# Two blocks on one core: the first modulation sums on TensorE, the levels of the linear attention on VectorE, and another distance between hT and the weights

## Chip, cores and metric

One core of one Trainium2 chip. The metric is the time on the device for one execution, in microseconds (us); it is given as the median of several runs. All weights are read from HBM in each execution, 228 MB of them.

## What is computed

256 tokens of width 1024 pass through two blocks. The first block is modulated by a condition vector; the second has a gated linear attention and a differential attention. Cut to what the change touches:

```python
mod = silu(cond) @ w_mod + b_mod                 # 1024 -> 9 * 1024
sh1, sc1, g1, sh2, sc2, g2, sh3, sc3, g3 = split(mod, 9)
h = rms_norm(x, ffn1_norm) * (1 + sc1) + sh1
x = x + 0.5 * g1 * (silu(h @ w_gate) * (h @ w_up)) @ w_down      # FFN1
# mixer: gated short convolution beside a state-space model (SSM); FFN2
proj = rms_norm(x, a_norm) @ w_in                # linear attention, 4 heads
q, k, v, g, z = split(proj)
log_a = log_sigmoid(z @ w_gate_up + b_gate) / 16
b = cumsum(log_a) within chunks of 64
# o_i = sum over j <= i of (q_i * exp(b_i - b_j)) . k_j  v_j, with a state between chunks
x = x + (rms_norm(o) * silu(g)) @ w_out
# then MLP, differential attention, MLP
```

Everything is float32.

## The kernel before

**Weights.** A stream (`Stream`) takes the weights in one fixed order, in pieces of 1 MB. Three stage buffers receive them by DMAs that SyncE issues; a piece that is consumed lets the next DMA go. `prep` splits a piece into two parts, so that a product of float32 values is made of three fast matmuls (`mm3`): ScalarE casts `wh` (L170, two halves), VectorE subtracts it to get `wl` (L172, two halves). The activations are split in the same way into `hTh` and `hTl` (L276, L277). The pairs lie in four slots and a fifth one (`grow`). `prep(upto, items)` prepares pieces as far as slots are free; `take(name, j, ahead)` prepares up to the piece asked for and `ahead` more, by default as many as slots allow. Instructions stand on each engine in the order in which the code emits them.

**The w_mod pieces.** They are in the same stream, four to each of the nine groups, the first eight (shift and scale of FFN1) ahead of all other weights. `mod_part` adds them on VectorE into `macc` (L839, L841: one input row times a scalar of `cact`, added; two for each piece). `mod_reduce` then sums `macc` over the partitions by eight matmuls with a column of ones (L862), and two small VectorE steps put bias and gain to it (`modf`).

**The start.** The x rows are normalised and transposed (`xnT`, L335); `evac` scales and shifts them with `modf` (L364 on ScalarE, L366 on VectorE) and splits them into hT. `turn` then makes FFN1's first gate and up products with tokens on the output's partitions, 24 matmuls for each of two pieces and two token halves; the rest of FFN1 (`up`, then `acc` for the down products) runs with the hidden units on the partitions. Beside that GpSimd works on the SSM (`powers`, `readout`, `tables`), and `Ssm.step(s)` spreads what TensorE and ScalarE do for it over the steps s of FFN1.

**The linear attention (`gla`).** TensorE makes v by `turn`, z, four chunks of q and k (0 to 3, `featb`), the last chunk of v (7) and four gate chunks (8 to 11). From z come the gates: two matmuls each, then Abs, Exp and Ln on ScalarE, a subtraction and a scan on VectorE give `b`. Within a chunk of 64 the products are built by levels (1, 2, 4, 8, 16, 32): `level_e` subtracts `b` at block borders, `exp` follows on ScalarE, `level_x` scales q and k on VectorE, `level_mm` multiplies on TensorE and copies into `AT` by a mask. `diagonal` gives the diagonal; `across_e` and what follows join the chunks of 64.

**Addresses.** Tiles are placed one behind the other in each partition; `pad` tiles shift what comes behind them. The weights' slots lie at 96 bytes modulo 512; hT lies at 32 and q's hT (differential attention) at 160.

Of the kernel before, what the change touches and what calls it, by code (L numbers as in the profile page):

```python
# [193 lines left out]
class Net:  # L194
# [219 lines left out]
    def turn(self, tail, evac, chunks, use):  # L414
# [5 lines left out]
        if tail is None:  # L420
            evac(0)
            evac(1)
        else:
            for part in tail.parts[0]:
                part()
            tail.post(0)
            early = len(tail.parts[1]) - tail.late
            for part in tail.parts[1][:early - 2]:
                part()
            S.prep(S.n_take + n_c)  # L430
            for part in tail.parts[1][early - 2:early]:
                part()
            evac(0)
            for part in tail.parts[1][early:]:
                part()
            S.prep(S.n_take + n_c)
            tail.post(1)
            if self.after_tail is not None:
                self.after_tail()
                self.after_tail = None  # L440
                S.prep(S.n_take + n_c)
        Ws = []
        for i in range(2):
            for c in range(n_c):
# [7 lines left out]
                if i == 0 and c == 1 and n_c > 2:  # L452
                    evac(1)
# [110 lines left out]
class Ssm:  # L564


    def __init__(self, N, p):
# [136 lines left out]
    def step(self, s):  # L704
# [3 lines left out]
        if 2 <= s <= 4:  # L708
            for b in ((0, 1), (2, 3, 4), (5, 6, 7))[s - 2]:
# [6 lines left out]
            if s == 4:  # L716
                self.readout()
                self.tables()
# [64 lines left out]
def build(N):  # L783
# [64 lines left out]
    def mod_reduce(g, new_bank, later=False):  # L848
# [15 lines left out]
        def finish():  # L864
            col = modf[:, 2 * blk + kind, :]
            nc.vector.tensor_tensor(out=col, in0=bank[:, 0:KD], in1=sv["b_mod"][:, g, :], op=ADD)
            if kind == 1:
                nc.vector.scalar_tensor_tensor(out=col, in0=col, scalar=1.0, in1=(G_FFN1, G_MIX, G_FFN2)[blk], op0=ADD, op1=MUL)

        if later:  # L870
            return finish
        finish()
# [28 lines left out]
    mod_reduce(1, lambda: N.bank_a("mod"))  # L901
    ssm.powers()
# [32 lines left out]
    def side1(s):  # L935
# [4 lines left out]
    tail = N.ffn(None, lambda i: N.evac_mod(pts[i], i, modf[:, 1, :], modf[:, 0, :], N.hT),  # L940
                 ("ffn1_w_gate", "ffn1_w_up"), "ffn1_w_down", 11, True, post_ffn1, side1, 1)
# [327 lines left out]
def gla(N, tail, evac, c):  # L1269
    nc, t, t2, take = N.nc, N.t, N.t2, N.take  # L1270
    ones, misc, ident = c["ones"], c["misc"], N.ident
    vt, gt, act = nc.vector.tensor_tensor, nc.gpsimd.tensor_tensor, nc.scalar.activation
# [28 lines left out]
    wz = [v3(w, KD) for w in take("a_z")]  # L1301
# [6 lines left out]
    def featb(ch, dst, scale):  # L1308
        ps = N.bank_u("qk")
        N.feat(take("a_in", ch), N.hT, v3(ps, 2))  # L1310
        N.S.free()
        act(out=flat(dst), in_=ps, func=AF.Copy, scale=scale)

    qT, kT = t2([4, S], "qT"), t2([4, S], "kT")
    featb(0, qT[:, 0:2, :], 128 ** -0.5)
    gp = []
    for h2 in range(2):
        ps = N.bank_a("gate")
        for k in range(2):
            h = 2 * h2 + k  # L1320
            nc.tensor.matmul(ps[:, S * k:S * k + S], wgu[:16, 128 * h:128 * h + 128], zT[:16, :], start=True, stop=True)
        gp.append(ps)
# [18 lines left out]
    def level_e(li):  # L1341
# [6 lines left out]
        gt(out=ev[:, :, 1, :], in0=bv[:, :, 1, :], in1=ref, op=SUB)  # L1348
        gt(out=ev[:, :, 0, :], in0=ref, in1=bv[:, :, 0, :], op=SUB)
# [51 lines left out]
    def across_e():  # L1401
# [62 lines left out]
    W = take("a_in", 8)  # L1464
    level_x(2)
    level_e(4)
    exp(Es[4])
    level_x(3)
    level_e(5)
    exp(Es[5])  # L1470
    gate_chunk(0, W)
    level_mm(2)
    level_mm(3)
    W = take("a_in", 9)
# [42 lines left out]
    for hp in range(2):  # L1517
        for i in range(2):
            av(i, hp)
    for hd in range(3):  # L1520
        gated(hd)
    nc.scalar.preload_act_table(AF.Silu)
    W = take("a_in", 11)
    ps = N.bank_u("vg")
    for i in range(2):
        N.tokm(W, N.hT, i, ps[:, CW * i:CW * i + CW])
    N.S.free()
    act(out=flat(sg[3]), in_=ps, func=AF.Silu)
# [63 lines left out]
def diff(N, tail, c):  # L1592
# [149 lines left out]
    def turn_o(p):  # L1742
# [8 lines left out]
        else:  # L1751
            if p == 2:
                N.pad("pad_tail", 128, N.pool2)
# [140 lines left out]
```

## Time and profile before

| | us |
|---|---|
| median of 3 runs | 1246.31 |
| the three runs | 1244.81 to 1246.57 |
| the profiled execution, its own time | 1243.52 |
| its span in the trace | 1241.8 |
| TensorE busy in it | 1140.0 |
| VectorE busy | 796.8 |
| ScalarE busy | 613.7 |
| GpSimd busy | 237.1 |

The span runs from the first to the last instruction; the execution's own time has 1.7 us more around it. Busy time of engines overlaps. A line number stands for the code that emits an instruction, a helper's line for all its callers (L248 is `mm3`). A name with an arrow, as `turn<-wh,hTh`, is the output tile and the inputs; for a matmul `128*128 128x256` are the loaded block and the streaming operand. One float32 matmul with float32 operands leaves two records, of the split ones one.

### The profile page before, as it was taken

Reading aid. Unit: us, or ns where it says so; the run is one execution under the profiler, and the core shown is the slowest. Engines: PE = TensorE matmul, PEld = TensorE weight load, DVE = VectorE, ACT = ScalarE, POOL = GpSimd, SP = SyncE. Lnnn points to the kernel's source line nnn. Section 1 sums busy time; section 2 is a strip of 40 time slices with the busy share of each in tenths; the row PEclk is TensorE's granted clock in tenths of the full one; section 3 lists DMA queues with packets and bytes.
Section 4 is the critical chain, followed back from the end, with each engine's and each line's share of the span. In section 5 each row is a group of like instructions: output and inputs, shape, how many; then the busy total and the mean of one; then the engine's idle time right before and its main releaser. Section 6 shows DMA issues by size and latency. Waiting matters only on the chain.

```text
span 1241.8 us, 18751 instructions
## 1 busy us (share of the span) xinstructions
PE 1140.0 (92%) x7780; PEld 1055.1 (85%) x7780; DVE 796.8 (64%) x934; ACT 613.7 (49%) x941; POOL 237.1 (19%) x304
## 2 busy tenths in 40 slices
PE   2689999989788899999697998999999899999998
PEld 2678998979777889997697988999989898899997
DVE  7698788677877855454567656544468776545441
ACT  3444443564265544444473656555456665645541
POOL 8994399401400000000214100000000000000000
PEclk9989999999789999999897999999999899899999
DMA  8598788436243765563144255556435333455540
GB/s 319 205 326 310 270 321 325 149 136 238 94 177 137 281 235 180 174 233 105 68 149 158 73 182 204 177 200 203 170 136 200 107 136 119 173 193 180 180 157 34
DMA packets 33093, 230.13 MB, mean 185 GB/s; under 512 B 3680, under 2 KB 4064, under 8 KB 5872
## 3 DMA queue, kind: packets, MB, share of 16 engines
q1 hardware_dynamic: 31536, 224.05, 50.5%
q10 hardware_dynamic: 1472, 4.88, 1.1%
q8 instruction: 61, 1.00, 0.3%
q14 instruction: 24, 0.20, 0.0%
HBM read 227.87 MB, written 1.05 MB: 184 GB/s over the span
## 4 chain that ended last, share of the span: by engine, by line
PE 68%; DVE 15%; ACT 7%; POOL 4%; DMA 3%; issue 3%; ACTq 0%; DVEq 0%; POOLq 0%
PE acc L248 27%; PE up L248 25%; PE turn L248 8%; DVE wl L172 7%; PE kqv L248 2%; ACT wh L170 2%; POOL s_small L612 1%; PE xnT L335 1%; POOL s_small L615 1%; DVE macc L841 1%; PE lev L1370 1%; DMA stage<-in_w 1%; DMA stage<-in_a_in 1%; ACT s_lag L734 1%; PE glu L248 1%
## 5 line engine op out<-in xcount | busy, mean ns | idle before, releaser
L172 DVE TENSOR_TENSOR wl<-stage,wh 128x1024 fp32r<-128x1024 f32 x351 | 429.5, 1270 | 144.2 <-ACT wh L170 144.2
L170 ACT CAST wh<-stage 128x1024 fp32r<-128x1024 f32 x351 | 347.2, 1044 | 147.1 <-PE acc L248 37.5
L248 PE MATMUL up<-hTh,wh 128*128 128x256 f32 x1024 | 288.1, 281 | 0.2 <-ACT s_end L715 0.2
L248 PE MATMUL up<-hTl,wh 128*128 128x256 f32 x1024 | 287.0, 280 | 0.0
L248 PE MATMUL up<-hTh,wl 128*128 128x256 f32 x1024 | 286.9, 280 | 0.0
L248 PEld LDWEIGHTS up<-hTh,wl 128*128 128x128 f32 x1024 | 195.4, 191 | 0.0
L248 PEld LDWEIGHTS up<-hTh,wh 128*128 128x128 f32 x1024 | 192.5, 188 | 2.4 <-ACT s_end L715 0.5
L248 PEld LDWEIGHTS up<-hTl,wh 128*128 128x128 f32 x1024 | 192.4, 188 | 1.6 <-issue 0.2
L248 PE MATMUL acc<-wh,hidh 128*128 128x512 f32 x288 | 116.6, 405 | 10.7 <-ACT hidh L276 5.4
L248 PE MATMUL acc<-wh,hidl 128*128 128x512 f32 x288 | 116.1, 403 | 9.8 <-DVE hidl L277 9.5
L248 PE MATMUL acc<-wl,hidh 128*128 128x512 f32 x288 | 115.6, 401 | 1.7 <-DVE wl L172 1.7
L248 PE MATMUL turn<-wh,hTh 128*128 128x256 f32 x320 | 92.4, 289 | 10.2 <-ACT hTh L276 10.2
L248 PE MATMUL turn<-wl,hTh 128*128 128x256 f32 x320 | 91.6, 286 | 1.7 <-DVE wl L172 1.7
L248 PE MATMUL acc<-wh,macc 128*128 128x512 f32 x288 | 93.1, 391 | 0.0
L248 PE MATMUL turn<-wh,hTl 128*128 128x256 f32 x320 | 91.9, 287 | 0.0
L841 DVE SCALAR_TENSOR_TENSOR macc<-stage,cact,macc 128x1024 f32<-128x1024 f32 x63 | 85.5, 1358 | 4.1 <-DMA stage<-in_w_mod 2.6
L248 PEld LDWEIGHTS acc<-wh,hidl 128*128 128x128 f32 x288 | 55.9, 194 | 24.1 <-DVE hidl L277 11.6
L248 PEld LDWEIGHTS acc<-wh,hidh 128*128 128x128 f32 x288 | 55.9, 194 | 23.5 <-ACT hidh L276 6.3
L248 PEld LDWEIGHTS turn<-wh,hTh 128*128 128x128 f32 x320 | 62.5, 195 | 11.0 <-ACT hTh L276 10.8
L248 PEld LDWEIGHTS acc<-wl,hidh 128*128 128x128 f32 x288 | 55.9, 194 | 13.7 <-DVE wl L172 3.1
L248 PEld LDWEIGHTS turn<-wl,hTh 128*128 128x128 f32 x320 | 62.5, 195 | 2.1 <-DVE wl L172 1.9
L248 PEld LDWEIGHTS acc<-wh,macc 128*128 128x128 f32 x288 | 54.1, 188 | 11.0
(401 smaller groups left out, 2023.4 us busy)
## 6 DMA issues: line engine op xcount, KB each, us to landing
stage<-in_w SPq DMA_DIRECT2D x64, 1024.0 KB, 4.8
stage<-in_w_mod SPq DMA_DIRECT2D x36, 1024.0 KB, 5.0
stage<-in_ffn_w_gate SPq DMA_DIRECT2D x22, 1024.0 KB, 4.8
stage<-in_ffn_w_up SPq DMA_DIRECT2D x22, 1024.0 KB, 4.8
stage<-in_ffn_w_down SPq DMA_DIRECT2D x22, 1024.0 KB, 4.8
stage<-in_a_in SPq DMA_DIRECT2D x12, 1024.0 KB, 5.1
stage<-in_w_in SPq DMA_DIRECT2D x8, 1024.0 KB, 5.1
stage<-in_w_kv SPq DMA_DIRECT2D x8, 1024.0 KB, 4.9
```

Of the source, the lines that this page charges most:

```text
L170: nc.scalar.copy(out=h[:, b:e], in_=st[:, b:e])
L172: nc.vector.tensor_tensor(out=lo[:, b:e], in0=st[:, b:e], in1=h[:, b:e].bitcast(F32), op=SUB)
L248: self.nc.tensor.matmul(out, lhs(l, k), rhs(r, k), start=first and n == 0, stop=last and n == 3 * n_k - 1)
L335: self.nc.tensor.transpose(out, src, self.ident)
L612: g.tensor_tensor(out=o, in0=x, in1=y, op=op)
L615: g.tensor_scalar(out=o, in0=x, scalar1=s1, scalar2=s2, op0=op0, op1=op1)
L734: nc.scalar.copy(out=self.lag[32 * i:32 * i + 32, 4 * b:4 * b + 4, 32 * i:128], in_=ks[:32, :, 0:128 - 32 * i])
L841: nc.vector.scalar_tensor_tensor(out=acc, in0=wv[:, k, :], scalar=cc, in1=acc, op0=MUL, op1=ADD)
L1370: nc.tensor.matmul(ps[:, 64 * e:64 * e + 64], ks[:, 128 * e:128 * e + 128], qs[:, 64 * e:64 * e + 64], start=True, stop=True)
```

## The change

- **w_mod, groups 0 and 1.** `mod_part` makes 16 matmuls for each of the eight pieces: a 128x128 block of the piece is loaded, one column of `cact` streams, and each result goes to a column of its own in one PSUM bank (`early`). `mod_early` sums these columns on VectorE and puts bias and gain to them. The other seven groups stay as they are.
- **Order at the start.** Six of the eight pieces (four before) are emitted ahead of the transposes. The first gate and up pieces are prepared behind the first evacuation, the second evacuation stands behind the first 24 `turn` matmuls, and the SSM's powers behind that. The SSM's memsets go from GpSimd to VectorE. Its `s_end` transposes, read-out and tables come one step of FFN1 later.
- **Linear attention.** `level_e` and the differences of `across_e` go from GpSimd to VectorE, two copies of `across_e` to ScalarE. The gate matmuls stand between the two halves of chunk 0. `take(..., 0)` at six places prepares nothing ahead, and `prep` is called later. Levels are emitted in pairs. The last gate chunk is split into its token halves, one ahead of the `av` products and one behind them.
- **Addresses.** Other sizes of four pads put hT, and q's hT, at 352 modulo 512: 256 from the weights. They were 64 away (on either side).

The core of the diff:

```diff
     def mod_part(g, c, st):
         wv = v3(st, 2)
+        if g < 2:
+            if c == 0:
+                early[g] = N.bank_a("mod")
+            for j in range(KD):
+                for k in range(2):
+                    nc.tensor.matmul(early[g][:, j * 8 + 2 * c + k:j * 8 + 2 * c + k + 1], wv[:, k, 128 * j:128 * j + 128],
+                                     cact[:, 2 * c + k:2 * c + k + 1], start=True, stop=True)
+            return
...
+    def mod_early(g):
+        tot = t([KD], "rs_sq", bufs=2)
+        nc.vector.tensor_reduce(out=tot, in_=v3(early[g][:, 0:64], KD), axis=AX.X, op=ADD)
+        col = modf[:, g, :]
+        nc.vector.tensor_tensor(out=col, in0=tot, in1=sv["b_mod"][:, g, :], op=ADD)
+        if g == 1:
+            nc.vector.scalar_tensor_tensor(out=col, in0=col, scalar=1.0, in1=G_FFN1, op0=ADD, op1=MUL)
...
     ssm.prepare()
     N.pad("pad_macc", 384)
-    St.prep(0, 4)
+    St.prep(0, 6)
     N.pad("pad_xn", 128)
     pts = [N.transp(N.normed(x[:, i, :])) for i in range(2)]
-    N.pad("pad_hT", 448)
+    N.pad("pad_hT", 256)
     N.hT = N.new_hT()
-    N.pad("pad_slots", 64)
+    N.pad("pad_slots", 256)
     nc.scalar.preload_act_table(AF.Silu)
-    shift = mod_reduce(0, lambda: N.bank_a("mod"), True)
+    mod_early(0)
     St.prep(0)
-    shift()
     nc.sync.dma_start(out=bc, in_=a["ssm_bc"])
-    St.prep(1)
-    mod_reduce(1, lambda: N.bank_a("mod"))
-    ssm.powers()
+    mod_early(1)
...
+    def evac_first(i):
+        N.evac_mod(pts[i], i, modf[:, 1, :], modf[:, 0, :], N.hT)
+        if i == 0:
+            St.prep(2)
+        else:
+            ssm.powers()
...
-        g.memset(p0, 0.0)
-        for c in range(2):
-            g.memset(self.out[c], 0.0)
-        g.memset(self.lag, 0.0)
+        for z in [p0] + self.out + [self.lag]:
+            N.nc.vector.memset(z, 0.0)
...
-        if 2 <= s <= 4:
-            for b in ((0, 1), (2, 3, 4), (5, 6, 7))[s - 2]:
+        if 3 <= s <= 5:
+            for b in ((0, 1), (2, 3, 4), (5, 6, 7))[s - 3]:
...
-    featb(0, qT[:, 0:2, :], 128 ** -0.5)
...
+    featb(0, qT[:, 0:2, :], 128 ** -0.5, gates, 0)
...
-        gt(out=ev[:, :, 1, :], in0=bv[:, :, 1, :], in1=ref, op=SUB)
-        gt(out=ev[:, :, 0, :], in0=ref, in1=bv[:, :, 0, :], op=SUB)
+        vt(out=ev[:, :, 1, :], in0=bv[:, :, 1, :], in1=ref, op=SUB)
+        vt(out=ev[:, :, 0, :], in0=ref, in1=bv[:, :, 0, :], op=SUB)
...
-    W = take("a_in", 7)
+    W = take("a_in", 7, 0)
     vt(out=kss[:, 2], in0=qf, in1=kf, op=MUL)
     level_x(0)
+    level_x(1)
     level_e(2)
     exp(Es[2])
-    level_x(1)
     level_e(3)
     exp(Es[3])
+    N.S.prep(10 ** 9)
...
-            N.pad("pad_hq", 448, N.pool2)
+            N.pad("pad_hq", 128, N.pool2)
...
-                N.pad("pad_tail", 128, N.pool2)
+                N.pad("pad_tail", 448, N.pool2)
```

How TensorE's instructions stand at the start of the program (`xnT` are the transposes of x, `turn` the first product of FFN1), before:

```order
L335 MATMUL xnT<-ident,xn 128x128 x16
L862 MATMUL mod<-ones,macc 128x1 x16
L248 MATMUL turn<-wh,hTh 128x256
L248 MATMUL turn<-wl,hTh 128x256
L248 MATMUL turn<-wh,hTl 128x256
```

and now:

```order
L835 MATMUL mod<-cact,stage 128x1 x96
L335 MATMUL xnT<-ident,xn 128x128 x16
L835 MATMUL mod<-cact,stage 128x1 x32
L248 MATMUL turn<-wh,hTh 128x256
L248 MATMUL turn<-wl,hTh 128x256
```

The 128 matmuls with `stage` stand ahead of the first `turn`, in place of 16 with `macc`; 96 of them are also ahead of the transposes.

ScalarE in the linear attention, from the DMA of the gate weights on (`wh` are casts of weight pieces, `E` the gate chain and the levels' factors), before:

```order
L1280 DMA hidf<-in_a_gate_up 16x512
L170 CAST wh<-stage 128x1024 x8
L1312 ACTIVATE qT<-qk 128x512
L1327 ACTIVATE E<-gate,pack 128x256 x4
L1328 ACT_TABLE_LOAD
L1328 ACTIVATE E<-E 128x1024
L1329 ACT_TABLE_LOAD
L1329 ACTIVATE E<-E 128x1024
L1333 ACT_TABLE_LOAD
L170 CAST wh<-stage 128x1024 x2
L1312 ACTIVATE qT<-qk 128x512
```

and now:

```order
L1294 DMA hidf<-in_a_gate_up 16x512
L1332 ACTIVATE qT<-qk 128x512
L1350 ACTIVATE E<-gate,pack 128x256 x4
L1351 ACT_TABLE_LOAD
L1351 ACTIVATE E<-E 128x1024
L1352 ACT_TABLE_LOAD
L1352 ACTIVATE E<-E 128x1024
L1356 ACT_TABLE_LOAD
L170 CAST wh<-stage 128x1024 x10
L1332 ACTIVATE qT<-qk 128x512
L170 CAST wh<-stage 128x1024 x2
```

Eight casts (chunks 1 to 3 and 7) that stood ahead of the first `qT` stand behind the gate chain, together with the next two.

VectorE at the same place, around the copy of z, before:

```order
L172 TENSOR_TENSOR wl<-stage,wh 128x1024 x6
L1306 COPY zT<-z 16x256
L172 TENSOR_TENSOR wl<-stage,wh 128x1024 x2
L1326 TENSOR_SCALAR E<-gate,pack 128x256 x4
L1330 TENSOR_TENSOR E<-E 128x1024
L1332 SCALAR_TENSOR_TENSOR b<-gate,E 128x1024
```

and now:

```order
L1320 COPY zT<-z 16x256
L1349 TENSOR_SCALAR E<-gate,pack 128x256 x4
L1353 TENSOR_TENSOR E<-E 128x1024
L1355 SCALAR_TENSOR_TENSOR b<-gate,E 128x1024
L172 TENSOR_TENSOR wl<-stage,wh 128x1024 x12
L1371 TENSOR_TENSOR E<-b 128x512
L1372 TENSOR_TENSOR E<-b 128x512
L1371 TENSOR_TENSOR E<-b 128x256x2
L1372 TENSOR_TENSOR E<-b 128x256x2
L172 TENSOR_TENSOR wl<-stage,wh 128x1024 x2
```

The scan (`b<-gate,E`) no longer has eight `wl` ahead of it at this place; behind it stand twelve `wl` instead of eight, and the first two levels' differences stand ahead of `ks`.

## Rows read from the trace of the kernel before

**Rows 1.** The page, part 4: the chain that ended last, shares by engine.

```profile
PE 68%; DVE 15%; ACT 7%; POOL 4%; DMA 3%; issue 3%; ACTq 0%; DVEq 0%; POOLq 0%
```

**Rows 2.** Timeline, TensorE at the start: start, us, engine, line, operation, output<-inputs, count [idle before].

```profile
22.64 3.65 PE L335 MATMUL xnT<-ident,xn 128*128 128x128 f32 x16 [22.64 <-POOL s_small L612]
26.08 3.41 PE L862 MATMUL mod<-ones,macc 128*128 128x1 f32 x16
...
43.75 0.58 PE L248 MATMUL turn<-wh,hTh 128*128 128x256 f32 x1 [6.28 <-ACT hTh L276]
```

**Rows 3.** Timeline of VectorE at the start.

```profile
6.26 6.39 DVE L839 TENSOR_SCALAR macc<-stage,cact 128x1024 f32<-128x1024 f32 x1 [6.26 <-DMA stage<-in_w_mod]
...
24.64 9.21 DVE L841 SCALAR_TENSOR_TENSOR macc<-stage,cact,macc 128x1024 f32<-128x1024 f32 x7
...
41.60 0.25 DVE L666 RECIPROCAL s_small<-s_small 128x16 f32<-128x16 f32 x1 [3.72 <-POOL s_small L612]
```

**Rows 4.** Timeline of ScalarE at the start.

```profile
37.98 1.50 ACT L364 ACTIVATE hm<-xnT,modf 128x128 f32<-128x128 f32 x4 [2.64 <-DVE modf L868]
43.08 1.14 ACT L276 CAST hTh<-hm 128x512 fp32r<-128x512 f32 x2 [3.60 <-DVE hm L366]
```

**Rows 5.** Timeline of TensorE in the mixer, one-column matmuls.

```profile
358.80 1.84 PE L862 MATMUL mod<-ones,macc 128*128 128x1 f32 x16
360.50 2.14 PE L1182 MATMUL ss<-ones,s_end 128*128 128x1 f32 x16
```

**Rows 6.** Stretches: from:to, length, busy us (instructions) by engine, granted clock, DMA share, GB/s.

```profile
230.00:300.00 70.00, 65.41 (x480) 60.74 (x478) 47.08 (x73) 41.71 (x73) 2.83 (x7) 0.98 0.45 160
362.10:365.40 3.30, 3.30 (x16) 3.30 (x17) 3.30 (x4) 2.63 (x3) 0.00 (x0) 0.50 0.31 79
665.80:672.50 6.70, 6.70 (x33) 6.70 (x33) 3.41 (x3) 3.74 (x6) 3.98 (x3) 0.50 0.00 0
```

**Rows 7.** Timeline of TensorE, first and last of closed runs of one kind.

```profile
60.79 0.29 PE L248 MATMUL up<-hTh,wh 128*128 128x256 f32 x1
...
365.81 0.28 PE L248 MATMUL glu<-hTl,wh 128*128 128x256 f32 x1
...
369.44 0.39 PE L248 MATMUL acc<-wh,s_tab 128*128 128x512 f32 x1
...
1139.68 0.39 PE L248 MATMUL acc<-wh,hidh 128*128 128x512 f32 x1
...
1143.76 0.28 PE L248 MATMUL up<-hTh,wh 128*128 128x256 f32 x1
...
1149.41 0.39 PE L248 MATMUL acc<-wh,macc 128*128 128x512 f32 x1
```

**Rows 8.** Timeline of TensorE in the linear attention.

```profile
662.37 3.54 PE L1385 MATMUL diag<-ones,ks 128*128 128x1 f32 x16 [7.06 <-DVE ks L1447]
665.78 7.07 PE L1370 MATMUL lev<-hidf,ks 128*128 128x64 f32 x32
```

**Rows 9.** Timeline of ScalarE in the linear attention.

```profile
633.05 0.59 ACT L1312 ACTIVATE qT<-qk 128x512 f32<-128x512 f32 x1
635.02 0.47 ACT L1327 ACTIVATE E<-gate,pack 128x256 f32<-128x256 f32 x1 [1.38 <-DVE E L1326]
...
637.96 1.28 ACT L1328 ACT_TABLE_LOAD   x1
...
644.00 2.00 ACT L170 CAST wh<-stage 128x1024 fp32r<-128x1024 f32 x2
```

**Rows 10.** Timeline of VectorE and GpSimd in the linear attention.

```profile
642.72 1.23 DVE L1330 TENSOR_TENSOR E<-E 128x1024 f32<-128x1024 f32 x1 [5.29 <-ACT E L1329]
644.05 2.29 DVE L1332 TENSOR_TENSOR_SCAN b<-gate,E 128x1024 f32<-128x1024 f32 x1
...
656.36 4.73 DVE L172 TENSOR_TENSOR wl<-stage,wh 128x1024 fp32r<-128x1024 f32 x4 [2.96 <-ACT wh L170]
...
652.28 2.02 POOL L1349 TENSOR_TENSOR E<-b 128x512 f32<-128x512 f32 x1
```

More of the change, by code (lines that the diff above doesn't have):

```diff
@@ L451, in turn @@
                     S.free()
-                if i == 0 and c == 1 and n_c > 2:
+                if i == 0 and (c == 1 and n_c > 2 or c == 0 and tail is None):
                     evac(1)
@@ L862, in mod_reduce @@
             nc.tensor.matmul(bank[:, k:k + 1], acc[:, 128 * k:128 * k + 128], ones[:, 0:1], start=True, stop=True)
[L864 to L872, printed above, removed]
+        col = modf[:, 2 * blk + kind, :]
+        nc.vector.tensor_tensor(out=col, in0=bank[:, 0:KD], in1=sv["b_mod"][:, g, :], op=ADD)
+        if kind == 1:
+            nc.vector.scalar_tensor_tensor(out=col, in0=col, scalar=1.0, in1=(None, G_MIX, G_FFN2)[blk], op0=ADD, op1=MUL)
     todo = list(range(2, 9))
@@ L1298, in gla @@
     nc.gpsimd.memset(step01.rearrange("p (n c) -> p n c", c=64)[:, :, 0:1], 0.0)
-    wz = [v3(w, KD) for w in take("a_z")]
+    wz = [v3(w, KD) for w in take("a_z", 0, 0)]
     zp = N.bank_u("z")[:16, :S]
@@ L1306, in gla, with featb, gates @@
     nc.vector.tensor_copy(out=zT[:16], in_=zp)
-    def featb(ch, dst, scale):
-        ps = N.bank_u("qk")
-        N.feat(take("a_in", ch), N.hT, v3(ps, 2))
+    def featb(ch, dst, scale, between=None, ahead=10 ** 9):
+        pv = v3(N.bank_u("qk"), 2)
+        W = take("a_in", ch, ahead)
+        wv = [v3(w, KD) for w in W]
+        for k in range(2):
+            cs = slice(128 * k, 128 * k + 128)
+            N.mm3(pv[:, k, :], lambda l, kk: wv[l][:, kk, cs], lambda r, kk: N.hT[r][:, kk, :], KD)
+            if k == 0 and between is not None:
+                between()
         N.S.free()
-        act(out=flat(dst), in_=ps, func=AF.Copy, scale=scale)
+        act(out=flat(dst), in_=flat(pv), func=AF.Copy, scale=scale)
     qT, kT = t2([4, S], "qT"), t2([4, S], "kT")
-    featb(0, qT[:, 0:2, :], 128 ** -0.5)
     gp = []
[L1317 to L1322, printed above, removed]
+    def gates():
+        for h2 in range(2):
+            ps = N.bank_a("gate")
+            for k in range(2):
+                h = 2 * h2 + k
+                nc.tensor.matmul(ps[:, S * k:S * k + S], wgu[:16, 128 * h:128 * h + 128], zT[:16, :], start=True, stop=True)
+            gp.append(ps)
+    featb(0, qT[:, 0:2, :], 128 ** -0.5, gates, 0)
     e1, mn = t2([4, S], "E", bufs=2), t2([4, S], "E", bufs=2)
@@ L1462, in gate_chunk @@
         tok_chunk(8 + hd, [sg[hd][:, i, :] for i in range(2)], W)
-    W = take("a_in", 8)
+    W = take("a_in", 8, 0)
     level_x(2)
+    level_x(3)
     level_e(4)
     exp(Es[4])
-    level_x(3)
     level_e(5)
     exp(Es[5])
+    N.S.prep(10 ** 9)
     gate_chunk(0, W)
@@ L1473, in gla @@
     level_mm(3)
-    W = take("a_in", 9)
+    W = take("a_in", 9, 0)
     level_x(4)
@@ L1479, in gla @@
         exp(E)
+    N.S.prep(10 ** 9)
     gate_chunk(1, W)
@@ L1486, in gla @@
     across()
+    W = take("a_in", 11)
+    last_gate = N.bank_u("vg")
+    N.tokm(W, N.hT, 0, last_gate[:, :CW])
     for hd in range(3):
@@ L1519, in gla @@
             av(i, hp)
+    N.tokm(W, N.hT, 1, last_gate[:, CW:])
+    N.S.free()
     for hd in range(3):
@@ L1522, in gla @@
     nc.scalar.preload_act_table(AF.Silu)
[L1523 to L1528, printed above, removed]
+    act(out=flat(sg[3]), in_=last_gate, func=AF.Silu)
     c["load"]("m0", t([D], "macc", bufs=2))
```

23 lines of the change are left out of this document (11 added, 12 removed).

## The prediction

> **What bounds the kernel now.** I read the page first: TensorE carries 68% of the chain of work that ended last [rows 1]. So a change counts where it moves TensorE's own work, or where TensorE stands and waits; a microsecond saved elsewhere counts only at such a place. Then I read the timeline by engine at the three places that the diff touches. At the start [rows 2 to 4] TensorE has done nothing but transposes and two reductions before its first `turn` matmul at 43.75; from there FFN1 runs nearly closed. In the linear attention [rows 8 to 10] one gap of 7.06 us stands before `diag`, put down to VectorE's `ks` (L1447). For the third part, the addresses, there is no wait to read at all: what matters is the distance from one matmul's start to the next in long runs without gaps [rows 7].
>
> **Part 1, shift and scale on TensorE.** Removed: 16 VectorE operations over 1024 elements. The first one takes 6.39 us beside GpSimd's memsets, the others 9.21 us for seven, 1.32 us each [rows 3]. Added: eight pieces of w_mod with 16 matmuls each, in which a 128x128 fp32 block is the loaded operand and one column streams. That form is in the trace: the reduction `mod<-ones,macc` is eight such matmuls, 16 records, 3.41 us [rows 2], so 0.426 us a matmul, with the records 213 ns apart, the pace of the lower clock level (1.2 GHz). The same form at 2.4 GHz is at 358.80: 16 records in about 1.7 us [rows 5].
>
> At which level would 128 of them run? The trace has a direct answer. From 358.80 to 362.5 TensorE did nothing but one-column matmuls, was busy without a gap, and entered at 2.4 GHz; the granted clock of the stretch behind it is 0.50 [rows 6]. And `diag` (one column) and `lev` (64 columns) ran 10 us without a gap at the slow pace, with 0.50 granted [rows 6, 8]. Ahead of the first `turn`, TensorE has nothing before them but transposes, whose records of 3.65 us for 16 are also those of the lower level [rows 2]. (The page writes a clock of 1.00 there, but the durations are twice those of the warm rows; I go by the durations.) So I take 1.2 GHz: 8 x 2 x 3.41 = 54.6 us.
>
> They lie on the path: the order shows 96 of them, then the transposes, then 32 more, all before the first `turn`. First piece landed 6.26 [rows 3]; 6.3 + 54.6 + 3.65 for the transposes = 64.5; sum, bias and gain some 0.5 (an estimate: small VectorE steps like the reciprocal, 0.25 us [rows 3], two or three of them): 65.0. Behind that stand ScalarE's four `hm` (1.50) and two `hTh` (1.14), then, newly behind instead of ahead, the casts of the first weights (2.00 for two) and VectorE's `wl` (4.73 for four, 1.18 each) [rows 4, 9, 10]: 65.0 + 1.5 + 1.14 + 1.0 + 1.18 = 69.8 for the first matmul with `wl`. The turn then has 96 matmuls at 0.118 us, 11.3, plus 1.7 for a first stretch still at the lower level: the first `up` at 82.8, where it was at 60.79 [rows 7]: **+22 us**. In this sum what the change gives back at the start is already counted: the 3.72 us that VectorE's reciprocal waited for GpSimd at 41.60 [rows 3] with the evacuations stuck behind it, and the wait for the second piece's `wl` within the turn. Nothing later absorbs it, since FFN1 is bound by TensorE and its weights are not what it waits for. Bounds: 18 if the end of it runs at the higher clock, 27 if the second piece's weights come late.
>
> Moved with it: the SSM's powers, read-out and tables start one FFN1 step later (steps 3 to 5 for 2 to 4). GpSimd has its tables done by 230 and is busy for 2.83 of the 70 us behind that [rows 6]: one step of about 17.5 us fits in what stands empty behind, and the first reader of the read-out has its own place at step 8. Costed at nothing; if that cover were too short, TensorE would wait some microseconds at `s_lag`, which is within the upper bound. The memsets on VectorE lie before its first work. Nothing either.
>
> **Part 2, levels of the linear attention.** GpSimd's level operations (2.02 us each [rows 10]) go to VectorE, where a 128x512 step takes about a third. They release `exp`, that released the casts of the last weights, and those stood ahead of `ks`: so the 7.06 us gap goes. What comes in its place: the casts of chunk 1 to 3 no longer stand ahead of the gate chain but behind it. Chunk 0 with the gates between its halves ends at about 632.5; from `qT` to the first table load were 4.91 us, of which 1.38 were a wait for the gates that no longer stands there, so 636.0; from that load to the first cast 637.96 to 644.00, 6.04 [rows 9], hence 642.1; the first cast 643.1. VectorE's subtraction starts with the end of the last Ln, 1.3 us before that, 640.8; with 1.23 and the scan's 2.29 it ends at 644.3, and `wl` at 645.5 [rows 10]. TensorE starts chunk 1 there, where it started at 633.3: a new gap of 13 us. Then four chunks, 22.0 us as before plus 1.7 for a cold start: 669.2; `diag` and the first two levels now at 2.4 GHz, half of 3.54 and 7.07 [rows 8]: 674.5; chunk 8, 5.5: 680.0, against 679.9 before. By this the old gap and the slow levels pay for the new one. The later levels now also wait for VectorE, which has 20 more operations between their inputs; I take **+3 us**, between -4 (the across part and the levels come earlier) and +8 (VectorE is late for levels 2 and 3). The last gate chunk, split around `av`, fills places without a gap: nothing, up to a microsecond either way.
>
> **Part 3, the addresses.** hT moves against the weights from 64 bytes (modulo 512) to 256; also for q. That touches 3072 `up` matmuls, 960 `turn`, 624 of `kqv` and `vg`: 4656. No row shows the distance 256 with 128-wide weights. The trace has two paces at 2.4 GHz and nothing between: `glu`, 32 matmuls from 365.81 to 369.44, 113.4 ns; `up`, 48 from 1143.76 to 1149.41, 117.7 ns [rows 7]. What the engines around do does not set which. The hidden states, at distance 0, run 512 columns in 227 ns (18 from 1139.68 to 1143.76), the fast pace; so the distance seems to count, and one far from what is now slow should run fast. If all took the fast pace the gain is at most 4656 x 4.3 ns = 20 us; some run fast already, so I take **-17**. The other end is all of them slow by one more such step, +20.
>
> The Trainium skill, "TensorE: Matmul & The Clock Gate", in Part 2, Step-by-step, says that loading weights has a read port of its own and takes no bandwidth from the streaming operand. By it no distance could matter. The two paces at one clock do not by themselves contradict that, since no run here shows what sets them; by it part 3 would be 0, which is rival (a).
>
> **Sum.** 1243.5 (the profiled execution's time) + 22 + 3 - 17 = 1251.5. The median of the runs stands 2.8 above the profiled one: **1254 us**, within 1246 to 1263 by the bounds of parts 1 and 2.
>
> **Rivals.** (a) The addresses give nothing: 1254 + 17 = 1271 (1263 to 1279). For: no wait in the trace names an address. Against: the two paces. (b) The distance 256 is worse than 64: up to 1254 + 37 = 1291. For: the trace does not have it. Against: a change to both sides of a pair that was slow already. (c) The other side: one-column matmuls, sustained long enough, do raise the clock. Then eight pieces take 27.3 us; 6.3 + 27.3 + 1.8 + 0.5 + 4.8 = 40.7 for the first `turn` with `wl`, and the turn runs warm throughout, 11.3: `up` at 52, 9 us earlier than now instead of 22 later; a piece can then wait for its transfer, which takes back some 3. So -6: 1246.3 - 6 + 3 - 17 = 1226 (1218 to 1235). It decides from the point at which the clock rises within the first 55 us: at half of them the sum is near 1240. For: 41 us in a row are longer than any such stretch in the trace. Against: [rows 5, 6] as above, where a warm clock was lost under exactly this work.
>
> The same page says in Part 1 that sustained activity releases the throttle; by it (c) would hold if this work counted as activity, and the row at 358.80 speaks against that.
>
> (d) Parts cancel: 18 for the start, -4 for the attention, 20 for the addresses: 1240 to 1249.
>
> **How the numbers follow.** Chances: the forecast 0.47, (a) 0.17, (b) 0.10, (c) 0.19, (d) 0.07. The range 1236 to 1287 leaves out most of (c), a third of (b) and little else. A measurement here can tell about 0.2%, 2.5 us. Faster by more: (c) and a part of (d), 0.21. Within: the rest of (d) and the lower edge of the forecast, 0.07. Slower: 0.72.
>
> **What would show it.** In the changed kernel: `mod<-cact,stage` as some 256 records 213 ns apart and the first `turn` near 69 (right) or 107 to 112 ns and the first `turn` near 40 (rival c). `up` at 113 ns from start to start throughout (part 3 right), still at 117.7 (a), or above (b). In the attention: no gap before `diag`, and a new one of 12 to 13 us before the second `qk` chunk, released by VectorE's `wl`; if that gap is small, the casts did not wait for the gate chain and the sum of part 2 is wrong. If TensorE waits before `s_lag`, the later step of the read-out was not covered.

## The result, and the profile after

| | us |
|---|---|
| before, median of 4 runs | 1245.56 |
| changed, median of 4 runs | 1279.22 (1276.66 to 1282.0) |
| ratio, 95% interval | 1.0271 (1.0246 to 1.0297) |
| forecast | 1254 |

The change is 33.7 us slower. The sign was forecast, the size was not: I had put it at 8 us.

Part 4 of the changed kernel's page, the chain that ended last, by engine and by line; compare [rows 1]:

```profile
PE 75%; DVE 13%; ACT 7%; DMA 3%; issue 2%; POOL 0%; ACTq 0%; SPq 0%; DVEq 0%; POOLq 0%
PE up L248 26%; PE acc L248 26%; PE turn L248 8%; DVE wl L172 6%; PE mod L835 4%; PE kqv L248 3%; ACT wh L170 2%; PE xnT L335 1%; PE proj L248 1%; DMA stage<-in_a_in 1%; DMA stage<-in_w 1%; PE s_lag L722 1%; PE ssm_w L1126 1%; PE s L1709 1%; PE mod L878 1%
```

TensorE's share has gone from 68% to 75%, GpSimd's 4% are gone, and 4% are new for the line of the added matmuls (L835). So most of it is TensorE's own time and not a wait that came in (one that did is shown below). Where it lies shows on TensorE's timeline. At the start (start, us, operation, count), to be read beside [rows 2]:

```profile
6.45 41.09 PE L835 MATMUL mod<-cact,stage 128*128 128x1 f32 x192 [6.45 <-DMA stage<-in_w_mod]
47.40 3.57 PE L335 MATMUL xnT<-ident,xn 128*128 128x128 f32 x16
50.81 10.58 PE L835 MATMUL mod<-cact,stage 128*128 128x1 f32 x64
65.67 0.58 PE L248 MATMUL turn<-wh,hTh 128*128 128x256 f32 x1 [4.28 <-ACT wh L170]
...
80.31 0.28 PE L248 MATMUL up<-hTh,wh 128*128 128x256 f32 x1
```

The first `turn` comes at 65.67 where it was at 43.75, +21.9; the first `up` at 80.31 where it was at 60.79, +19.5. From there to the end of FFN2 the distance to the kernel before grows slowly on the whole, to 25 us: the long runs themselves have become slower. Two rows of the same timeline in the last MLP, the first `up` of a run of 48 and the `acc` behind it, to be read beside the last two of [rows 7]:

```profile
1142.15 0.28 PE L248 MATMUL up<-hTh,wh 128*128 128x256 f32 x1
...
1147.90 0.40 PE L248 MATMUL acc<-wh,macc 128*128 128x512 f32 x1
```

48 matmuls in 5.75 us, 119.8 ns each, where it was 117.7. In all long runs of 256 columns at the higher clock (some 5000 matmuls) it is now 119.9 ns, with hardly any spread; the two paces of before, 113.4 and 117.7, do not occur. In the linear attention, beside [rows 8]:

```profile
669.31 0.58 PE L248 MATMUL qk<-hTh,wh 128*128 128x256 f32 x1 [10.59 <-ACT wh L170]
...
671.72 0.58 PE L248 MATMUL qk<-hTh,wl 128*128 128x256 f32 x1 [1.62 <-DVE wl L172]
...
696.21 1.84 PE L1408 MATMUL diag<-ones,ks 128*128 128x1 f32 x16
697.91 5.82 PE L1393 MATMUL lev<-hidf,ks 128*128 128x64 f32 x32
```

The 7.06 us before `diag` are gone, and a wait of 10.59 us for ScalarE's cast and of 1.62 for `wl` stands ahead of the second `qk` chunk. When the attention's `turn` began the two kernels stood 25.6 us apart (603.22 and 628.78), at `diag` 33.8, behind the attention 31 to 32. So the start has lost some 20 us, the runs up to the attention 6, the attention 6, and what follows about 1 (there the distance moves between 31 and 35 us; the spans end 32.7 apart). No part as a whole has gained.

### The profile page after: what moved, and what is told of

Read it like the earlier page. It is cut to its first block, busy times and chain, and to the rows that moved or that the text cites. A ratio compares the mean times of both kernels' runs of the same rounds, so it can differ in the third digit from the quotient of the medians.

```text
span 1274.5 us, 19174 instructions
## 1 busy us (share of the span) xinstructions
PE 1197.0 (94%) x8004; PEld 1111.7 (87%) x8004; DVE 782.2 (61%) x941; ACT 614.8 (48%) x944; POOL 189.2 (15%) x280
## 4 chain that ended last, share of the span: by engine, by line
PE 75%; DVE 13%; ACT 7%; DMA 3%; issue 2%; POOL 0%; ACTq 0%; SPq 0%; DVEq 0%; POOLq 0%
PE up L248 26%; PE acc L248 26%; PE turn L248 8%; DVE wl L172 6%; PE mod L835 4%; PE kqv L248 3%; ACT wh L170 2%; PE xnT L335 1%; PE proj L248 1%; DMA stage<-in_a_in 1%; DMA stage<-in_w 1%; PE s_lag L722 1%; PE ssm_w L1126 1%; PE s L1709 1%; PE mod L878 1%
## 5 line engine op out<-in xcount | busy, mean ns | idle before, releaser
L172 DVE TENSOR_TENSOR wl<-stage,wh 128x1024 fp32r<-128x1024 f32 x351 | 424.4, 1255 | 139.2 <-ACT wh L170 138.9
L248 PE MATMUL up<-hTh,wh 128*128 128x256 f32 x1024 | 291.1, 284 | 0.0
L248 PEld LDWEIGHTS up<-hTh,wh 128*128 128x128 f32 x1024 | 196.4, 192 | 2.2 <-ACT wh L170 0.5
L248 PEld LDWEIGHTS up<-hTl,wh 128*128 128x128 f32 x1024 | 196.4, 192 | 1.8 <-issue 0.5
L248 PE MATMUL acc<-wh,hidh 128*128 128x512 f32 x288 | 117.1, 407 | 8.3 <-ACT wh L170 4.2
L849 DVE SCALAR_TENSOR_TENSOR macc<-stage,cact,macc 128x1024 f32<-128x1024 f32 x49 | 67.3, 1373 | 1.1
```

The source lines that it names most:

```text
L172: nc.vector.tensor_tensor(out=lo[:, b:e], in0=st[:, b:e], in1=h[:, b:e].bitcast(F32), op=SUB)
L248: self.nc.tensor.matmul(out, lhs(l, k), rhs(r, k), start=first and n == 0, stop=last and n == 3 * n_k - 1)
L849: nc.vector.scalar_tensor_tensor(out=acc, in0=wv[:, k, :], scalar=cc, in1=acc, op0=MUL, op1=ADD)
```

## Experiments: one part at a time

Four kernels were made from the one before. Their times stand against runs of the kernel before on the same chip (median 1242.89).

**The start alone.** All of the diff up to `evac_first`, without the pads and the linear attention:

```diff
+        if g < 2:
...
+                    nc.tensor.matmul(early[g][:, j * 8 + 2 * c + k:j * 8 + 2 * c + k + 1], wv[:, k, 128 * j:128 * j + 128],
+                                     cact[:, 2 * c + k:2 * c + k + 1], start=True, stop=True)
...
-    St.prep(0, 4)
+    St.prep(0, 6)
```

> The kernel before with the start of the changed kernel alone (first two modulation sums on TensorE, its order, the later SSM steps); addresses and linear attention as before. Theory (one-column matmuls run at 1.2 GHz, 54 us of them on the path): the first up matmul at about 80 us instead of 60.8, and the time 18 to 22 us above before, near 1265. Rival (the 34 us of the whole change come mostly from the addresses, and the start's loss is given back in FFN1): within 8 us of before, near 1250.

Measured: 1266.17, ratio 1.0183 (1.0157 to 1.0208), so +23 us. TensorE's timeline at its start:

```profile
6.57 41.09 PE L835 MATMUL mod<-cact,stage 128*128 128x1 f32 x192 [6.57 <-DMA stage<-in_w_mod]
47.52 3.65 PE L335 MATMUL xnT<-ident,xn 128*128 128x128 f32 x16
50.97 13.65 PE L835 MATMUL mod<-cact,stage 128*128 128x1 f32 x64
68.91 0.58 PE L248 MATMUL turn<-wh,hTh 128*128 128x256 f32 x1 [4.29 <-ACT wh L170]
...
82.80 0.28 PE L248 MATMUL up<-hTh,wh 128*128 128x256 f32 x1
```

192 records in 41.1 us and 64 in 13.65, 213 ns each from beginning to end; the first `up` at 82.80. The rival falls: nothing of it is given back in FFN1. The s_lag matmuls, which the later read-out might have held up, do not wait.

**The addresses alone.**

```diff
-    N.pad("pad_hT", 448)
+    N.pad("pad_hT", 256)
...
-    N.pad("pad_slots", 64)
+    N.pad("pad_slots", 256)
...
-            N.pad("pad_hq", 448, N.pool2)
+            N.pad("pad_hq", 128, N.pool2)
...
-                N.pad("pad_tail", 128, N.pool2)
+                N.pad("pad_tail", 448, N.pool2)
```

> The kernel before with the four pads of the changed kernel alone: hT 256 bytes from the weights modulo 512. Theory (the distance sets the pace): every 256-column matmul at 120.0 ns from start to start where up had 117.0 and turn 117.5 on average and proj, qk and glu 113.4; 3072 x 2.9 + 960 x 2.4 + 624 x 2.9 + 480 x 6.4 ns = 16 us if all of it is on the path, so 1255 to 1262. Rival (the pace came from the other edits, the address has no part): 1246, with up at 117 ns.

Measured: 1252.44, ratio 1.0073 (1.0046 to 1.0100), +9 us. Two rows of TensorE's timeline, an `up` run and what follows it:

```profile
1137.93 0.28 PE L248 MATMUL up<-hTh,wh 128*128 128x256 f32 x1
...
1143.68 0.40 PE L248 MATMUL acc<-wh,hidh 128*128 128x512 f32 x1
```

48 in 5.75 us again: 119.8 ns, with nothing changed but four pads. By the counts this should cost 16 us; the medians are 9.5 us apart and the spans of the two traces 6.1 (1247.9 and 1241.8). Two things in these traces go the other way. TensorE's waits of more than 0.4 us that end behind 44 us sum to 63.0 us in the trace of before and to 56.7 here; that they shrink because the engines that it waits for did not get slower is my reading, and no run tests it. And the granted clock was 0.50 for 79 us in place of 92; but this share varies between executions of one kernel too (in the nine runs of the kernel before the mean granted clock was 0.951 to 0.963).

The rule of the Trainium skill that the prediction weighed ("TensorE: Matmul & The Clock Gate", Part 2, Step-by-step: loading weights takes nothing from the streaming operand's reads) does not agree with this run, if it is read as "addresses cannot matter": where hT lies does set the pace, by up to 6.5 ns in 120 (113.4 and 119.9, table below). That it is the bandwidth of these reads that is lost, no run shows.

**The linear attention alone.** All hunks of `gla`:

```diff
-    featb(0, qT[:, 0:2, :], 128 ** -0.5)
+    featb(0, qT[:, 0:2, :], 128 ** -0.5, gates, 0)
...
-        gt(out=ev[:, :, 1, :], in0=bv[:, :, 1, :], in1=ref, op=SUB)
+        vt(out=ev[:, :, 1, :], in0=bv[:, :, 1, :], in1=ref, op=SUB)
...
-    W = take("a_in", 7)
+    W = take("a_in", 7, 0)
```

> The kernel before with the new linear attention alone. Theory (a wait of about 12 us for the weights of chunk 1 behind the gate chain takes the place of the 7 us gap before diag, and diag and the first levels get faster only in part): 4 to 7 us above before, near 1251. Rival (the attention's loss in the whole change comes from the new addresses in it): within 2 us of before or below.

Measured: 1251.22, ratio 1.0067 (1.0044 to 1.0090), +8 us. TensorE's timeline:

```profile
643.59 0.58 PE L248 MATMUL qk<-hTh,wh 128*128 128x256 f32 x1 [10.59 <-ACT wh L170]
...
646.00 0.58 PE L248 MATMUL qk<-hTh,wl 128*128 128x256 f32 x1 [1.62 <-DVE wl L172]
...
669.61 1.95 PE L1394 MATMUL diag<-ones,ks 128*128 128x1 f32 x16
671.44 5.20 PE L1379 MATMUL lev<-hidf,ks 128*128 128x64 f32 x32
679.07 0.58 PE L248 MATMUL vg<-wh,hTh 128*128 128x256 f32 x1 [2.43 <-ACT macc L1405]
```

The new wait is there (10.59 and 1.62, the forecast had 13 in one), and `diag` starts at 669.61, where the sum had 669.2. What the sum missed comes behind it. The clock of two stretches (length, busy by engine, granted clock):

```profile
671.50:676.60 5.10, 5.10 (x33) 4.95 (x32) 3.94 (x6) 2.12 (x3) 0.00 (x0) 0.70 0.21 87
679.10:687.00 7.90, 7.90 (x50) 7.90 (x50) 7.70 (x10) 0.00 (x0) 0.00 (x0) 0.71 0.39 135
```

`diag` ran fast (1.95 us in place of 3.54), but the levels behind it lost the clock (0.70 in the mean, 5.20 us where half of 7.07 was expected), and the gate chunk behind them ran partly without it (0.71). Between them stands a wait of 2.43 us for ScalarE to copy the v chunk out of its bank (`macc`, L1405). On ScalarE's timeline the copy stands behind the `exp` of the next levels, which waited for VectorE's differences, and behind casts:

```profile
674.33 2.26 ACT L1361 ACTIVATE E<-E 128x1024 f32<-128x1024 f32 x2 [6.86 <-DVE E L1358]
676.50 1.98 ACT L170 CAST wh<-stage 128x1024 fp32r<-128x1024 f32 x2
678.38 0.64 ACT L1405 COPY macc<-vg 128x256 f32<-128x256 f32 x2
```

**Nothing but distance 0.**

```diff
-    N.pad("pad_hT", 448)
+    N.pad("pad_hT", 512)
...
-    N.pad("pad_slots", 64)
...
-            N.pad("pad_hq", 448, N.pool2)
+            N.pad("pad_hq", 384, N.pool2)
...
-                N.pad("pad_tail", 128, N.pool2)
+                N.pad("pad_tail", 192, N.pool2)
```

> The kernel before with hT, and q's hT, at the same place as the weights modulo 512 (distance 0 where before has 64 and the changed kernel 256), nothing else. Theory (distance 0 is the fast one, as in the 512-column matmuls of the hidden states, 227 ns): all 256-column matmuls at 113.4 ns, 4656 x 3.6 ns = 15 to 17 us below before, near 1229. Rival (any distance but that of before is slower, or distance does not matter): 1246 or above.

Measured: 1255.13, ratio 1.0084 (1.0054 to 1.0113). Slower, and the theory that I still held here fell. An `up` run in its trace:

```profile
1121.03 0.28 PE L248 MATMUL up<-hTh,wh 128*128 128x256 f32 x1
...
1126.78 0.40 PE L248 MATMUL acc<-wh,macc 128*128 128x512 f32 x1
```

Again 119.8 ns, at the very distance at which 512-column matmuls of the hidden states run at 227 ns, twice 113.4 [rows 7]. So here the pace of one shape at a distance says nothing of another shape at the same distance.

The three single parts multiply to 1.0326, with an interval (roots of the summed squares) that reaches down to 1.028; the whole change has 1.0271 (1.0246 to 1.0297). They add, or nearly: the whole is about 7 us under the sum of its parts, of which 2.5 are seen at the start, below.

## Experiments: what stands behind each part

**The start with 128 columns in place of one.** The load of each 128x128 block stays, the column of `cact` is streamed 128 times, and the sums are collected in PSUM:

```diff
-                    nc.tensor.matmul(early[g][:, j * 8 + 2 * c + k:j * 8 + 2 * c + k + 1], wv[:, k, 128 * j:128 * j + 128],
-                                     cact[:, 2 * c + k:2 * c + k + 1], start=True, stop=True)
+                    nc.tensor.matmul(early[g][j // 4][:, 128 * (j % 4):128 * (j % 4) + 128], wv[:, k, 128 * j:128 * j + 128],
+                                     cact[:, 2 * c + k:2 * c + k + 1].to_broadcast([128, 128]),
+                                     start=c == 0 and k == 0 and j % 4 == 0, stop=c == 3 and k == 1 and j % 4 == 3)
```

> As start_only, but each of the 128 matmuls streams the column of cact 128 times (sums collected in PSUM, the first of the 128 equal columns is used). The load of the 128x128 block is the same. Theory (the start is dear because one-column matmuls leave TensorE at 1.2 GHz): the wider stream raises the clock, 16 records take about 1.8 us instead of 3.4, the eight pieces are bound by their transfers, the first up matmul comes at 50 to 58 us instead of 82.8 and the time is 24 to 32 us under start_only, below the kernel before. Rival (the loads alone cost that much, or the clock stays at 1.2 GHz with these too): the first up at 80 or later, time 1264 or more.

Measured: 1240.47, ratio 0.9962 (0.9946 to 0.9978) against before (1244.59), 26 to 28 us under the start with one column (by the medians and by the ratios; the two were measured on different chips). Its timeline and two stretches:

```profile
6.70 24.51 PE L835 MATMUL mod<-cact,stage 128*128 128x128 f32 x192 [6.70 <-DMA stage<-in_w_mod]
31.05 1.91 PE L335 MATMUL xnT<-ident,xn 128*128 128x128 f32 x16
32.79 7.31 PE L835 MATMUL mod<-cact,stage 128*128 128x128 f32 x64
44.13 0.58 PE L248 MATMUL turn<-wh,hTh 128*128 128x256 f32 x1 [4.03 <-ACT wh L170]
...
58.83 0.28 PE L248 MATMUL up<-hTh,wh 128*128 128x256 f32 x1
```

```profile
6.70:12.60 5.90, 5.90 (x28) 5.90 (x29) 2.41 (x2) 0.00 (x0) 4.40 (x21) 1.00 1.02 430
12.70:31.00 18.30, 18.30 (x166) 18.30 (x166) 2.42 (x8) 6.09 (x14) 4.91 (x23) 1.00 0.79 273
```

28 records in the first 5.9 us, 211 ns each; then 166 in 18.3 us, 110 ns each. (The page writes 1.00 for the first stretch too, but the trace's first record of the clock is at 12.64 us; the durations tell the levels apart.) TensorE streamed 128 times the columns, and the first 192 records took 24.5 us where they took 41.1. The first `up` is at 58.83, just behind the 50 to 58 that was expected. So the price of part 1 was the clock, not the loads, not the transfers and not the order.

**The linear attention with weights prepared ahead.** As the attention alone, but `take` and `featb` without the limit of 0 and without the three late `prep` calls:

```diff
-    wz = [v3(w, KD) for w in take("a_z", 0, 0)]
+    wz = [v3(w, KD) for w in take("a_z")]
...
-    featb(0, qT[:, 0:2, :], 128 ** -0.5, gates, 0)
+    featb(0, qT[:, 0:2, :], 128 ** -0.5, gates)
...
-    W = take("a_in", 7, 0)
+    W = take("a_in", 7)
...
-    N.S.prep(10 ** 9)
```

> As gla_only, but weights are prepared ahead as in the kernel before (no limit on what take prepares, no late prep calls); the levels stay on VectorE, the gate matmuls inside chunk 0, the last gate chunk split. Theory (the loss of gla_only is the wait for chunk 1's weights behind the gate chain): that wait of 10 to 12 us is gone, the gap before diag is 4 us or less, and the time is 8 to 12 us under gla_only, 1239 to 1243. Rival (VectorE has too much to do with the levels on it): the gap before diag or the waits between levels grow, and it stays within 3 us of gla_only.

Measured: 1248.78, ratio 1.0038 (1.0022 to 1.0054); the attention alone had 1.0067. By the ratios that is 3 to 4 us less, where the theory had 8 to 12: somewhat under half of the loss is gone. TensorE's timeline:

```profile
630.66 2.43 PE L1328 MATMUL gate<-zT,hidf 16*128 16x256 f32 x8 [3.38 <-issue]
...
665.37 2.83 PE L1394 MATMUL diag<-ones,ks 128*128 128x1 f32 x16 [4.04 <-DVE ks L1456]
```

The wait ahead of chunk 1 is gone. But the gates, now between the halves of chunk 0, wait 3.38 us themselves: they read `zT`, whose copy stands on VectorE behind six `wl` of the weights prepared ahead and ends at 630.56. VectorE's timeline:

```profile
623.34 6.90 DVE L172 TENSOR_TENSOR wl<-stage,wh 128x1024 fp32r<-128x1024 f32 x6 [11.46 <-ACT wh L170]
630.16 0.40 DVE L1306 COPY zT<-z 16x256 f32<-16x256 f32 x1
```

The order of the changed kernel avoids that wait with the limit of 0 and pays 12 us for it. What makes up the rest of the loss that is left was not taken apart.

**The levels on VectorE, and nothing else.**

```diff
-        gt(out=ev[:, :, 1, :], in0=bv[:, :, 1, :], in1=ref, op=SUB)
-        gt(out=ev[:, :, 0, :], in0=ref, in1=bv[:, :, 0, :], op=SUB)
+        vt(out=ev[:, :, 1, :], in0=bv[:, :, 1, :], in1=ref, op=SUB)
+        vt(out=ev[:, :, 0, :], in0=ref, in1=bv[:, :, 0, :], op=SUB)
```

> The kernel before with only the level and across differences moved from GpSimd to VectorE (two across copies to ScalarE); casts, gates, takes and the last gate chunk in the order of before. Theory (the move itself is good, gla_only and gla_eager lose by the order around it): VectorE's four differences take about 2.8 us behind the scan where GpSimd had 7.8, the exp come earlier, the gap before diag shrinks from 7.06 to 2 us or less, no new gap appears; 3 to 7 us below before. Rival (VectorE is what the levels wait for): gaps before the later levels, within 2 us of before or above.

Measured: 1244.99, ratio 1.0005 (0.9989 to 1.0021): no change, where 3 to 7 us less were expected. The gap before `diag` is 6.25 us in place of 7.06:

```profile
664.21 3.54 PE L1385 MATMUL diag<-ones,ks 128*128 128x1 f32 x16 [6.25 <-DVE ks L1447]
```

VectorE and ScalarE ahead of it:

```profile
646.91 2.29 DVE L1332 TENSOR_TENSOR_SCAN b<-gate,E 128x1024 f32<-128x1024 f32 x1
649.12 4.61 DVE L172 TENSOR_TENSOR wl<-stage,wh 128x1024 fp32r<-128x1024 f32 x4
...
655.44 0.69 DVE L1349 TENSOR_TENSOR E<-b 128x512 f32<-128x512 f32 x1
658.19 4.74 DVE L172 TENSOR_TENSOR wl<-stage,wh 128x1024 fp32r<-128x1024 f32 x4 [2.06 <-ACT wh L170]
```

```profile
655.02 2.21 ACT L1352 ACTIVATE E<-E 128x1024 f32<-128x1024 f32 x2 [3.29 <-DVE E L1349]
657.13 1.97 ACT L170 CAST wh<-stage 128x1024 fp32r<-128x1024 f32 x2
```

The differences take 0.69 us each where GpSimd had 2.02 [rows 10], and the last is done at 656.1. But GpSimd could begin right behind the scan, beside four `wl` on VectorE; now the differences stand behind these four on the same engine (which take 4.61 us here and took 7.14 beside GpSimd in the trace of before). From the end of the scan to the last difference it was 7.9 us and is 6.9. The `exp`, the casts, the next four `wl` and `ks` follow as before, in a row, 0.8 us earlier.

**Other distances.** Each is the kernel before with other sizes of the same four pads, as in the distance 0:

> The kernel before with hT, and q's hT, 96 bytes from the weights modulo 512 (dist_0 had 0, the changed kernel 256, before 64 on either side). Theory A (what counts is the distance modulo 128: 0 is slow at 120.0 ns, about half of it fast): 113 to 118 ns, time within 4 us of before. Theory B (what counts is being within 64 bytes of 448 or 64 modulo 512): 120 ns and about 1254.

> The kernel before with hT 128 bytes from the weights modulo 512. Theory A (distance modulo 128 counts): all 256-column matmuls at 120.0 ns as with 0 and 256. Theory B (the nearest of 64 and 448 counts, or any distance but 0 and 256 is fast): between 113 and 118 ns.

> The kernel before with hT, and q's hT, 32 bytes behind the weights modulo 512. Of the distances so far 0, 96, 128 and 256 run at 118 to 121 ns and only 64 on either side at 113 to 118. Theory (64 on either side is a best of its own): 118 to 120 ns. Rival (near but not 0 is good): 113 to 117 ns.

> The kernel before with hT, and q's hT, 32 bytes ahead of the weights modulo 512 (480), the mirror of dist_32. Theory (64 on either side is a best of its own): 118 to 120 ns. Rival (near but not 0 is good): 113 to 117 ns for up.

Mean from one start to the next at the higher clock in each trace, worked out from the records (some 3016 pairs of `up`, 950 of `turn`, 189 of `qk`), in ns:

| hT's place less the weights' (modulo 512) | `up` | `turn` | `qk` | time, us | ratio |
|---|---|---|---|---|---|
| 448 (before; q's hT 64) | 117.0 | 117.4 | 113.4 | 1242.9 to 1245.8 | 1 |
| 480 | 118.3 | 117.1 | 118.3 | 1246.28 (one run) | |
| 0 | 119.9 | 119.9 | 119.9 | 1255.13 | 1.0084 (1.0054 to 1.0113) |
| 32 | 116.7 | 118.3 | 116.7 | 1247.70 (one run) | |
| 96 | 120.1 | 118.0 | 119.9 | 1253.43 | 1.0079 (1.0051 to 1.0107) |
| 128 | 119.5 | 118.9 | 118.7 | 1251.89 (one run) | |
| 256 (addresses alone) | 119.9 | 119.9 | 119.9 | 1252.44 | 1.0073 (1.0046 to 1.0100) |

No distance tried is faster than that of before. 96 went as theory B had it (`up` 120.1, 1253); 128 went as neither, near 119 and spread out, where A had a fixed 120.0. 32 behind has `up` at the pace of before and `turn` slower, 32 ahead the other way round; so 64 is not a best of its own, but nothing near it gains. What within TensorE or the memory makes the pace stays open; distances of 160 to 224 and 288 to 416 were not tried. In all these kernels it is hT that moved, and the weights stayed at 96 modulo 512. So the runs do not tell the distance between the two from hT's own place; "distance" is the name for what was changed.

The two paces of `up` in the trace of before, at one distance, go with what stands ahead of a run. A run of `up` keeps one pace from its beginning to its end. All 34 that stand directly behind `acc` matmuls go at 117.8 ns, as the one at 1143.76 [rows 7]; all four that stand directly behind `turn` go at 113.6 to 113.7. The first of these four, with the instruction ahead of it and the one behind its 48 matmuls:

```profile
60.67 0.28 PE L248 MATMUL turn<-wh,hTl 128*128 128x256 f32 x1
60.79 0.29 PE L248 MATMUL up<-hTh,wh 128*128 128x256 f32 x1
...
66.25 0.60 PE L335 MATMUL hidT<-ident,hidf 128*128 128x128 f32 x4
```

Runs behind transposes or other work have either pace, and in the start alone one behind `turn` has 117.7; so what in the work ahead decides is open. At 0 and 256 the runs behind `acc` and those behind `turn` all go at 119.8 to 120.0.

**A version that beats both.** The start with 128 columns, the first gate piece cast ahead of the first evacuation, the levels on VectorE alone, the addresses of before:

```diff
+    St.prep(1)
     mod_early(1)
```

> start_128col with the weights of the first gate piece cast ahead of the first evacuation, and with gla_vec's linear attention; addresses as in the kernel before. If the parts add: the 4 us that start_128col gained, up to 4 more for the wait before the first turn matmul, and gla_vec's 3 to 7: 1230 to 1236 where before has about 1244. Rival (what is gained early is lost at a later wait, as weights arrive no earlier): 1239 or more.

Measured: 1238.27 (1234.61 to 1243.3), ratio 0.9951 (0.9927 to 0.9975), short of the 1230 to 1236 that were expected. Its first `turn` and first `up`:

```profile
42.01 0.38 PE L248 MATMUL turn<-wh,hTh 128*128 128x256 f32 x1 [3.32 <-ACT hTh L276]
...
55.43 0.28 PE L248 MATMUL up<-hTh,wh 128*128 128x256 f32 x1
```

The early cast gave 3.4 us at the first `up` (55.43 for 58.83), of which at most 1 to 2.5 are left at the end; the interval includes what the 128 columns alone gave, so even that is not shown. The levels on VectorE add nothing that can be measured, as they did alone.

## Why the prediction was right and wrong, step by step

- **Part 1, +22 us: right.** One-column matmuls at 1.2 GHz, read from the durations and from the stretch at 358.80 [rows 5, 6] in which this work lost the clock. The start alone has 256 records in 54.7 us (54.6 in the sum), the first `up` at 82.80, the number of the sum, and costs 23 us. In the whole change it is 19.5 at the same place, as the section on the hardware below tells.
- **Part 3, -17 us: wrong, in sign.** It is +9 alone. The step that failed is "so the distance seems to count, and one far from what is now slow should run fast". That the place of hT counts holds, but by luck: the rows that I took it from do not show it. `glu` (113.4) and `up` (117.7) [rows 7] stand at the same distance, and the two paces of `up` in that trace go with what stands ahead of a run. The second half was drawn from the 512-column rows at distance 0, and the run at distance 0 shows that 256 columns are slow just there. No row had the shape at the distance; I had a bound for that (all slow by one more step of 4.3 ns, +20) and gave the case 0.10, against the equal bound on the other side with 0.47. What it measured is 2.9 ns of a step for `up` in the mean. The count of 4656 was short as well: it leaves out the 480 matmuls of `proj`, `qk` and `glu`, which also read hT and went from 113.4 to 119.9. From -17 to +9 are 26 us, about the whole distance from 1254 to 1279. Parts 1 and 2 alone cost 1 and 5 us more than forecast, and the whole change about 7 less than its parts, so these errors nearly cancel.
- **Part 2, +3 us: right in its mechanism, too small.** The new wait, its place and its length came as in the sum (`diag` at 669.61 against 669.2). The term that was mis-sized is what pays for it: "`diag` and the first two levels now at 2.4 GHz" and chunk 8 in 5.5 us, 674.5 and 680.0. They took until 676.64 and, after a wait of 2.43 that I had not counted, until 687: the clock was lost within the levels, which is what my own reading of [rows 6, 8] for part 1 should have told me for part 2.
- **The rivals.** (b), the distance 256 worse than 64, is what happened, with half its price. (a) fell with the addresses alone. (c) fell: 41 us of one-column matmuls in a row did not raise the clock. Its price came out about right with the 128 columns, which do raise it: 4 us under before, where (c) had 6 for the start. That is luck, for two errors cancel. The first `up` came at 58.8 and not at 52. Some 4.7 us of that lie ahead of the evacuation, mostly since the first 28 records ran at 1.2 GHz and the others took 110 ns in place of 106.6. The other 2.1 lie in the `turn`, which took 13.4 us in place of 11.3: TensorE lost the clock in the wait of 4.03 us for the casts, a wait that the sum had. But the 3 us that (c) let a late transfer take back were not taken back.
- **The cover.** The SSM's later steps cost nothing, as forecast: no wait at s_lag in any of these traces.

## What to carry to other kernels

A sum moved to an idle TensorE is only as cheap as the clock that it leaves: look for a stretch in which that very shape ran long, and see what the clock did behind it; if it fell, try a wider streaming operand, which here cost next to nothing: 110 ns a record with 128 columns, against 106 with one at the same clock [rows 5]. What the place of an operand in memory costs has to be read for each shape by itself: here a row of one shape gave neither sign nor size for another, so an address that no row shows is bounded evenly on both sides and not taken at the hopeful end. And when a late operand is moved forward by holding back weights, price the wait of the next chunk first: the held weights come back as a gap of their own.

## What the runs showed of the hardware

In the whole change the transposes at 47.40 stood between one-column matmuls, and behind them the clock rose and fell again. Two stretches of its trace behind the transposes, length, busy us (records) by engine, granted clock:

```profile
50.80:54.10 3.30, 3.30 (x33) 3.30 (x31) 0.00 (x0) 0.00 (x0) 0.00 (x0) 1.00 0.30 122
54.20:61.30 7.10, 7.10 (x35) 7.10 (x34) 0.00 (x0) 0.00 (x0) 0.00 (x0) 0.50 0.43 148
```

The 16 transposes took 3.57 us, the pace of the lower level; then come 33 records in 3.3 us at a granted 1.00, then 35 in 7.1 us at 0.50. The work in the two stretches is the same, one-column matmuls without a gap. So the clock rose behind the transposes of 128 columns in this execution, and the one-column work lost it again. In the start alone, with the same order, it did not rise behind them (64 records in 13.65 us there, 10.58 here): why it rose in one kernel and not in the other, and whether the transposes are what raised it, no run shows. It makes 2 to 3 us at this place. The Trainium skill, "TensorE: Matmul & The Clock Gate", Part 4, says that the full clock does not engage for transposes. The rise right behind them in this execution speaks against it; the start alone and the kernel before, whose one-column records behind the transposes are 213 ns apart [rows 2], agree with it.

A pace that hardly varies was the other surprise: at distances 0 and 256 the middle eight tenths of 3016 `up` matmuls lie within 1 ns of 120, while at 96 and 128 they spread over 9 and 5 ns, and at 64 they go at two paces some 4 ns apart.
